# Layer 1 weights fetched a step ahead, squares added by two engines, and dense bias tables in a two-layer hybrid attention kernel

## The chip, the cores and the metric

The kernel runs on one core of a Trainium2 chip. The time is device time in microseconds (us) of one launch, as the median over several runs. The engines are TensorE (PE), VectorE (DVE), ScalarE (ACT), GpSimd (POOL) and SyncE (SP), which here issues nearly all DMAs. "SPq" in a row is SP's DMA queue, where a row stands for the issue of a transfer, not for its landing.

## What is computed

One sample with 1024 latent tokens (a 16 x 64 grid) and 256 context tokens goes through two layers of width 1024. Each layer is attention and a SwiGLU network, each behind a modulated RMS norm (scale and shift come from the conditioning vector, `ada_params`). Layer 0 attends with eight heads in a neighbourhood with a table of relative position biases, and with eight grouped-query heads; layer 1 uses differential attention.

```python
def rms_norm(x, gain=None):
    y = xf * lax.rsqrt(jnp.mean(xf * xf, axis=-1, keepdims=True) + EPS)
def ada_params(cond, w, b):
    m = jax.nn.silu(cond) @ w + b
    return jnp.split(m[..., None, :], N_MOD, axis=-1)
# neighbourhood attention of layer 0, per grid row
s_win = einsum('bhqd,bhrqjd->bhqrj', q_r, k_win) * scale + bias
s_ctx = einsum('bhqd,bhkd->bhqk', q_r, kc) * scale
# differential attention of layer 1
s1 = einsum('bhqd,bhkd->bhqk', a1, k1) * scale
s2 = einsum('bhqd,bhkd->bhqk', a2, k2) * scale
p = softmax(s1) - lam * softmax(s2)
# feed-forward
(silu(h @ w_gate) * (h @ w_up)) @ w_down
```

## The kernel before

Activations lie transposed, features on the partitions, in eight tiles of 128 features, and in three blocks of tokens: block 0 is the context (256), blocks 1 and 2 hold 512 latent tokens each. Every product is three matmuls (`mm3`, L181 to L183): both operands are split into a high and a low part (hh, hl for activations, wh, wl for weights), and high x high, low x high and high x low are summed in PSUM. A weight chunk of 128 x 1024 is fetched by SP (L171), its high part is cast by ACT (L172), and its low part is the difference, on POOL or DVE (L173).

The order of instructions on each engine is set by a scheduler from the order of the code; `high_priority` moves work ahead, and `later()` gives work the lowest priority, so that it fills what others leave. Each engine runs its own list strictly in order, and SP issues its DMAs in order too: a transfer that waits for a buffer holds those behind it.

The stages that matter here:

- **Layer 0's projections** (up to 405 us). Eight chunks of query and key weights (ch 0 to 7) are multiplied; meanwhile the row maxima of the scores that the softmax needs are taken (L432 matmul, L410 reduction from PSUM; L471 transposes the result). Beside that, a modulation vector is built: `ada_acc` fetches eight 512 KB pieces of `ada_w` (L207) and accumulates them on DVE (L210, L214), and `ada_sum` sums over the partitions with eight one-column matmuls for each of two conditions (L235; the trace records each twice). Beside that too, `tables` builds the bias tables of the neighbourhood heads: it fetches rows of the padded bias (L630), adds a mask on POOL (L631) and stores to DRAM (L634). The stored rows have a pitch of 127, and the attention reads them back skewed, in pieces of 64 floats.
- **Layer 0's attention**: S^T matmuls (L853, L854), exponentials, and value matmuls (L888 to L891).
- **Down projection of layer 0 and the norm into layer 1**: the last group of SwiGLU products is added to x on DVE (L993); ACT squares x (L322), POOL adds the squares up (L323), a matmul with ones sums over the partitions (L329), and `norm_apply` makes the products x * rstd (L343, DVE), the scale and shift (L344, ACT) and the split (L164, ACT and L165, DVE).
- **Layer 1's projections** (1990 to 2500 us): for four groups g, first the keys (kind 1), then the queries (kind 0), each with two weight chunks w1 and w2. In the code both are fetched at the head of their step. After each step sixteen stores put the rotated keys or queries into DRAM (L1211; ks, qs). Then come the V weights (L1221). In between runs the "far" part: pairs of matmuls (L1063, L1064) for the log-sum-exp of the scores, each with a DVE maximum (L1065) and an ACT exponential (L1066); its q and k are fetched back from qs and ks (L1095 to L1102). How many pairs are put between the projection matmuls is set by `far`.

Of the kernel before, what the change touches and what calls it, by code (L numbers as in the profile page):

```python
# [17 lines left out]
P = 128  # L18
D = 1024
KD = 8  # L20
# [6 lines left out]
RPW = 127  # L27
RPN = 15 * RPW
# [24 lines left out]
def kernel(ctx: ExitStack, tc: tile.TileContext, xT, cond, ada_w, ada_b, win0, wv0, wout0, rp, rpf, qg, kg,  # L53
# [78 lines left out]
    sk = [dram([8, 64 * RPN + 2048], f"sk{i}") for i in range(2)]  # L132
# [18 lines left out]
    def skew(i, h, dr0, n):  # L151
        o = 63 + dr0 * RPW
        v = sk[i][h, o : o + 64 * (RPN - 1)].rearrange("(c n) -> c n", c=64)
        return v[:, : n * RPW].rearrange("c (u y) -> c u y", y=RPW)[:, :, :GW]

# [11 lines left out]
    def load_w(src, view=None, eng=None):  # L167
        raw = wpool.tile([P, 1024], F32, tag="wl", bufs=5, name=nm("wr"))
# [7 lines left out]
    def load_wchunk(src, eng=None):  # L176
        hi, lo = load_w(src, eng=eng, view=("p (k m) -> p k m", dict(k=KD)))
        return hi.rearrange("p (k m) -> p k m", k=KD), lo.rearrange("p (k m) -> p k m", k=KD)
# [146 lines left out]
    def norm_rstd(pool, ssq, w, pstag, tb=None):  # L325
        pst = ps(*pstag)
        parts = ssq if isinstance(ssq, list) else [ssq]
        for i, x in enumerate(parts):
            nc.tensor.matmul(pst[:, :w], ones, x, start=i == 0, stop=i == len(parts) - 1)  # L329
# [155 lines left out]
    with sbuf("hp0", 8) as hp, sbuf("a10", 8) as ap:  # L485
# [134 lines left out]
        cmt = ap.tile([P, 2, RPW], F32, tag="cmt", bufs=1, name="cmt")  # L620

        def tables(i, h):

            for d0, d1 in ((0, 8), (8, 15)):
                n = d1 - d0
                T = ap.tile([P, 8, RPW], F32, tag="aw", bufs=3, name=nm("sk"))[:, 0:n, :]
                T2 = T.rearrange("p u y -> p (u y)")
                for j in range(2):
                    src = (rpf, rp)[i][h + j : h + j + 1, d0 * RPW : d1 * RPW].to_broadcast([64, n * RPW])
                    nc.sync.dma_start(T2[64 * j : 64 * j + 64], src)  # L630
                nc.gpsimd.tensor_add(T, T, cmt[:, i : i + 1, :].to_broadcast([P, n, RPW]))  # L631
                for j in range(2):
                    dst = sk[i][h + j, : 64 * RPN].rearrange("(c n) -> c n", c=64)[:, d0 * RPW : d1 * RPW]
                    nc.sync.dma_start(dst, T2[64 * j : 64 * j + 64])  # L634

# [79 lines left out]
        for ch in range(8):  # L715
# [756 lines left out]
```

## Time and profile before

| quantity | value |
|---|---|
| median of 3 runs | 3656.18 us (3655.86 to 3661.64) |
| profiled execution | 3658.97 us, of it the span 3657.2 us |
| PE busy | 3415.5 us, 93% of the span |
| DVE busy | 2218.4 us, 61% |
| ACT busy | 1422.3 us, 39% |
| POOL busy | 825.2 us, 23% |
| DMA | 394.51 MB, 198081 packets, 57692 of them under 512 B |

The profile records each instruction of one execution. A wait is the idle time of an engine ahead of an instruction, with the instruction that ended it. The granted clock is the share of TensorE's full clock (2.4 GHz) that it ran at: 0.5 is the lower level, 1.2 GHz. Where two matmuls stand next to each other, the distance of their starts is the cost, since the second begins before the first one's recorded end.

### The profile page before, as it was taken

The page shows a single profiled execution, that of the slowest core. Times are in us where ns is not written, and L with a number is a line of the kernel's source. Part 1 is how long each engine was busy: PE and PEld are TensorE (multiplying, and loading weights), DVE is VectorE, ACT ScalarE, POOL GpSimd, SP SyncE. Part 2 cuts the span into 40 slices and gives each one's busy share as a digit, 9 for nine tenths or more (in the row PEclk, how much of TensorE's full clock was granted, in tenths as well). Part 3 has the DMA queues.
Part 4 walks back from the last instruction along what each step waited for, and adds up shares of the span by engine and source line. Part 5 has one row for each costly group of instructions (what it writes and reads, how often), then busy time and mean ns, then how long its engine had stood idle before and what let it go on. Part 6 is the DMA issues. An engine that isn't in the chain of part 4 may idle for free.

```text
span 3657.2 us, 43706 instructions
## 1 busy us (share of the span) xinstructions
PE 3415.5 (93%) x16044; PEld 2783.9 (76%) x16044; DVE 2218.4 (61%) x3555; ACT 1422.3 (39%) x2862; POOL 825.2 (23%) x622
## 2 busy tenths in 40 slices
PE   6799699988999999999998899899999999999997
PEld 4588577766888888888886678787666888888886
DVE  7767388887755555554336366787998533433335
ACT  4431067666441111111115254797777421111112
POOL 3212177766220000000003322002332200000002
PEclk8899789999999999999999999999999999999999
DMA  5276764374413333231112553646442211111111
GB/s 212 78 241 223 219 136 103 87 142 97 165 52 98 104 104 98 93 98 47 35 41 87 135 140 100 201 149 189 125 127 91 98 47 50 49 53 47 47 47 64
DMA packets 198081, 394.51 MB, mean 108 GB/s; under 512 B 57692, under 2 KB 99216, under 8 KB 197866
## 3 DMA queue, kind: packets, MB, share of 16 engines
q1 hardware_dynamic: 196074, 388.62, 36.0%
q0 software_dynamic: 1792, 3.10, 0.2%
q8 instruction: 126, 2.06, 0.2%
q14 instruction: 89, 0.73, 0.1%
HBM read 317.03 MB, written 74.61 MB: 107 GB/s over the span
## 4 chain that ended last, share of the span: by engine, by line
PE 74%; DVE 10%; ACT 5%; POOL 3%; issue 3%; DMA 3%; SPq 1%; POOLq 0%; DVEq 0%; ACTq 0%
PE psd L181 6%; PE psd L182 6%; PE psd L183 6%; PE psg L181 5%; PE psg L182 5%; PE psg L183 5%; PE psu L183 4%; PE psu L181 4%; PE psu L182 4%; PE psm L183 4%; PE psm L182 4%; PE psm L181 4%; PE pst L1318 2%; PE psq L1063 2%; PE pst L1319 2%
## 5 line engine op out<-in xcount | busy, mean ns | idle before, releaser
L173 POOL TENSOR_TENSOR wl<-wr,wh 128x1024 fp32r<-128x1024 f32 x69 | 168.0, 2435 | 1521.7 <-ACT wh L172 1315.4
L172 ACT CAST wh<-wr 128x1024 fp32r<-128x1024 f32 x193 | 202.2, 1049 | 761.7 <-PE psd L182 305.7
L993 DVE SCALAR_TENSOR_TENSOR x<-psd,mods,x 128x512 f32<-128x512 f32 (+1 forms) x448 | 301.3, 686 | 190.7 <-PE psd L183 190.4
L1027 DVE TENSOR_TENSOR sg<-sg,psu 128x512 f32<-128x512 f32 (+1 forms) x110 | 69.6, 634 | 484.4 <-PE psu L183 477.9
L181 PE MATMUL psd<-ah,wh 128*128 128x512 f32 (+1 forms) x896 | 331.3, 370 | 8.8 <-DVE x L993 6.8
L182 PE MATMUL psd<-al,wh 128*128 128x512 f32 (+1 forms) x896 | 328.3, 366 | 0.0
L183 PE MATMUL psd<-ah,wl 128*128 128x512 f32 (+1 forms) x896 | 326.9, 366 | 0.8 <-DVE wl L173 0.7
L181 PE MATMUL psg<-hh,wh 128*128 128x512 f32 (+1 forms) x880 | 326.2, 371 | 0.9 <-ACT sg L1024 0.9
L183 PE MATMUL psg<-hh,wl 128*128 128x512 f32 (+1 forms) x880 | 325.3, 370 | 0.1
L182 PE MATMUL psg<-hl,wh 128*128 128x512 f32 (+1 forms) x880 | 325.0, 369 | 0.0
L183 PE MATMUL psu<-hh,wl 128*128 128x512 f32 (+1 forms) x880 | 323.8, 368 | 0.5 <-POOL wl L173 0.5
L181 PE MATMUL psu<-hh,wh 128*128 128x512 f32 (+1 forms) x880 | 324.1, 368 | 0.0
L182 PE MATMUL psu<-hl,wh 128*128 128x512 f32 (+1 forms) x880 | 323.6, 368 | 0.0
L173 DVE TENSOR_TENSOR wl<-wr,wh 128x1024 fp32r<-128x1024 f32 x124 | 156.0, 1258 | 220.7 <-ACT wh L172 204.8
L1065 DVE TENSOR_REDUCE st<-psq 128x1 f32<-128x512 f32 (+1 forms) x384 | 219.4, 596 | 58.3 <-PE psq L1064 53.5
L1066 ACT ACTIVATE psq<-psq,st 128x512 f32<-128x512 f32 (+1 forms) x384 | 226.8, 594 | 65.0 <-DVE st L1065 61.3
L181 PE MATMUL psm<-hh,wh 128*128 128x512 f32 (+1 forms) x584 | 219.2, 376 | 25.7 <-ACT wh L172 18.4
L849 POOL TENSOR_TENSOR pl<-sb,ph 128x512 fp32r<-128x512 f32 (+1 forms) x144 | 203.5, 1420 | 91.9 <-ACT ph L848 60.2
L182 PE MATMUL psm<-hl,wh 128*128 128x512 f32 (+1 forms) x584 | 217.4, 373 | 6.5 <-DVE hl L349 4.7
L183 PE MATMUL psm<-hh,wl 128*128 128x512 f32 (+1 forms) x584 | 217.9, 373 | 3.7 <-POOL wl L173 3.7
L181 PEld LDWEIGHTS psd<-ah,wh 128*128 128x128 f32 x896 | 169.4, 189 | 44.0 <-DVE x L993 13.5
L1024 ACT ACTIVATE sg<-psg 128x512 f32<-128x512 f32 (+1 forms) x110 | 60.5, 552 | 344.4 <-PE psg L183 344.4
(276 smaller groups left out, 8331.2 us busy)
## 6 DMA issues: line engine op xcount, KB each, us to landing
aw<-in_ada_w SPq DMA_DIRECT2D x112, 512.0 KB
wr<-in_wg SPq DMA_DIRECT2D x44, 512.0 KB
wr<-in_wu SPq DMA_DIRECT2D x44, 512.0 KB
wr<-in_wd SPq DMA_DIRECT2D x44, 512.0 KB
k<-ks SPq DMA_DIRECT2D x32, 640.0 KB
wr<-in_wout SPq DMA_DIRECT2D x32, 512.0 KB
q<-qs SPq DMA_DIRECT2D x32, 512.0 KB
k<-ks SPq DMA_DIRECT2D x48, 320.0 KB
```

The lines of the kernel that those rows point to most:

```text
L172: nc.scalar.copy(hi, raw)
L173: (eng or nc.gpsimd).tensor_sub(lo, raw, f(hi))
L181: nc.tensor.matmul(o, ah, bh, start=start, stop=False)
L182: nc.tensor.matmul(o, ah, bl, start=False, stop=False)
L183: nc.tensor.matmul(o, al, bh, start=False, stop=stop)
L849: (nc.vector if npb[0] % LOD == 0 else nc.gpsimd).tensor_sub(lo, e, f(hi))
L993: nc.vector.scalar_tensor_tensor(xv, pst, mods[:, l, ci, 40 + oc : 41 + oc], xv, op0=ALU.mult, op1=ALU.add)
L1063: nc.tensor.matmul(p1, q2[:, a * P : a * P + P], k2[:, k0 : k0 + kw], start=True, stop=False)
L1065: nc.vector.tensor_reduce(st[:, 0, a, j : j + 1], p1, axis=AX.X, op=ALU.max, negate=True)
L1066: after_table(nc.scalar.activation(p1, p1, AF.Exp, bias=st[:, 0, a, j : j + 1], accum_out=st[:, 1, a, j : j + 1]))
L1318: nc.tensor.matmul(o, ks[c][1][:, kk], qs[c][1][:, c0 : c0 + 512], start=True, stop=False)
L1319: nc.tensor.matmul(o, ks[c][0][:, kk], qs[c][0][:, c0 : c0 + 512], start=False, stop=True)
```

## The change

- `load_w` takes a raw buffer from outside; in the down projection the raw buffers of a group are taken before the first load.
- In layer 0, the bias tables come in dense from the host (`tabT`, `tabQ`: rows of 15 x 64 for each of the 64 grid columns). `tables` is now one load, one POOL add of 960 columns and one store for two heads, where it was two pieces with two loads and two stores each. The attention reads contiguous rows.
- In layer 0's projections, the last `ada_acc` no longer stands under `later()`, and its sum comes at chunk 6 where it was at chunk 4.
- In the norm into layer 1 and in the last norm, every other square addition goes to DVE (`nc.vector if oc % 2 else None`).
- The ones matmul of block 2 gets a lower priority (`behind=70`).
- The first two weight chunks of layer 1 are fetched in the last down projection (`first_w`); after that each step fetches the next step's w1 at its head and the next step's w2 in its middle, and the last step fetches the first V weights (`vw1`).

```diff
-        raw = wpool.tile([P, 1024], F32, tag="wl", bufs=5, name=nm("wr"))
+    def load_w(src, view=None, eng=None, raw=None):
+        raw = wpool.tile([P, 1024], F32, tag="wl", bufs=5, name=nm("wr")) if raw is None else raw
...
+    def norm_rstd(pool, ssq, w, pstag, tb=None, behind=0):
...
+            with tc.high_priority(-behind):
+                nc.tensor.matmul(pst[:, :w], ones, x, start=i == 0, stop=i == len(parts) - 1)
...
-            for d0, d1 in ((0, 8), (8, 15)):
-                n = d1 - d0
-                T = ap.tile([P, 8, RPW], F32, tag="aw", bufs=3, name=nm("sk"))[:, 0:n, :]
...
+            T = ap.tile([P, 15, GW], F32, tag="aw", bufs=3, name=nm("sk"))
+            r = slice(64 * h, 64 * h + P)
+            nc.sync.dma_start(T.rearrange("p u y -> p (u y)"), (tabT, tabQ)[i][r])
+            nc.gpsimd.tensor_add(T, T, cmt[:, i : i + 1, :].to_broadcast([P, 15, GW]))
+            nc.sync.dma_start(sk[i][r], T.rearrange("p u y -> p (u y)"))
...
-            if ch in (1, 4):
+            if ch in (1, 6):
                 ada_sum(*pend_ada, qmt)
             if ch == 1:
-                with later():
-                    pend_ada = ada_acc(ap, *adas.pop(0))
+                pend_ada = ada_acc(ap, *adas.pop(0))
...
+            if l == 0:
+                first_w.append(load_wchunk(win1[8], nc.vector))
+                first_w.append(load_wchunk(win1[9], nc.vector, fp.tile([P, NT], F32, tag="al", bufs=4, name="wr1")[:, :1024]))
...
-                    sumsq_add(fp, sv, one(oc, blk), oc == 0, ("ah", NT, 4))
+                    sumsq_add(fp, sv, one(oc, blk), oc == 0, ("ah", NT, 4), nc.vector if oc % 2 else None)
...
-                rstd = norm_rstd(fp, sv, w, S1, 4)
+                rstd = norm_rstd(fp, sv, w, S1, 4, 70 if b == 2 else 0)
...
-                        w1 = load_wchunk(win1[kind * 8 + 2 * g], None if g or not kind else nc.vector)
-                        w2 = load_wchunk(win1[kind * 8 + 2 * g + 1], None if g or not kind else nc.vector)
+                        w1, w2 = ws
+                        nxt = order1[2 * g + 2 - kind] if 2 * g + 2 - kind < 8 else None
+                        ws = [load_wchunk(win1[nxt])] if nxt is not None else []
+                        if nxt is None:
+                            vw1(0, 0)
...
+                            if b == (0 if kind else 2):
+                                if nxt is not None:
+                                    ws.append(load_wchunk(win1[nxt + 1]))
+                                else:
+                                    vw1(0, 2)
...
-                for k0 in range(0, KD, 2):
...
+                for k0 in range(4 * (1 - g), KD, 2):
+                    vw1(g, k0)
```

How this moves instructions is seen in the order of each engine. PE, end of layer 0's projections, before (`psm` are projections, `acc` the modulation, `km`, `qm` the maxima's operands):

```order
L182 MATMUL psm_3628<-hl_538,wh_3533 128x512
L183 MATMUL psm_3628<-hh_537,wl_3532 128x512
L235 MATMUL psq_3216<-cst,acc_2710 128x1 x8
L432 MATMUL psq_3268<-km_1342,qm_2877 128x512
L432 MATMUL psq_3271<-km_1342,qm_2877 128x256
L235 MATMUL psq_3216<-cst,acc_2711 128x1 x8
L432 MATMUL psq_3274<-km_1342,qm_2877 128x512
```

Behind these follow 49 more L432 and two L471, and then the first S^T matmul. The same place after the change:

```order
L179 MATMUL psm_3564<-hl_538,wh_3469 128x512
L180 MATMUL psm_3564<-hh_537,wl_3468 128x512
L430 MATMUL psq_3589<-km_1342,qm_3287 128x512
L430 MATMUL psq_3592<-km_1342,qm_3287 128x256
L430 MATMUL psq_3595<-km_1342,qm_3287 128x512
L430 MATMUL psq_3598<-km_1342,qm_3287 128x512
L430 MATMUL psq_3601<-km_1342,qm_3287 128x256
L430 MATMUL psq_3604<-km_1342,qm_3287 128x512
L430 MATMUL psq_3607<-km_1342,qm_3287 128x512
L430 MATMUL psq_3668<-km_1342,qm_3287 128x256
L430 MATMUL psq_3671<-km_1342,qm_3288 128x512
L844 MATMUL pst_3675<-t_714_3653,t_716_3659 128x256
```

Nine maxima stand between the last projection matmul and the first S^T matmul (L844); the modulation sums and the other maxima have moved up among the projections.

SP, layer 1, between the key stores and the query stores of group 1 (`wr` is a weight; the second one is w2 of group 2's keys), after the change:

```order
L1232 DMA ks_93<-t_3177_16822 32x1280
L168 DMA wr_17051<-in_win 128x1024
L1232 DMA qs_92<-t_3206_17057 32x1024
L1232 DMA qs_92<-t_3207_17058 32x1024
L168 DMA wr_17226<-in_win 128x1024
L1232 DMA qs_92<-t_3208_17059 32x1024
L1232 DMA qs_92<-t_3209_17060 32x1024
```

The second weight stands behind two of the query stores. In group 0 (first weight of the next step, then the stores) it stands ahead of them, after the change:

```order
L1232 DMA ks_93<-t_3131_16448 32x1280
L168 DMA wr_16753<-in_win 128x1024
L1232 DMA qs_92<-t_3152_16659 32x1024
L1232 DMA qs_92<-t_3153_16660 32x1024
```

Before, the same weight (w2 of group 1's keys) stood behind all sixteen, and this is the end of them:

```order
L1211 DMA qs_92<-t_3160_16719 32x1024
L1211 DMA qs_92<-t_3161_16720 32x1024
L171 DMA wr_16871<-in_win 128x1024
```

DVE, the norm into layer 1, the end of block 2's squares, before (no square addition on DVE; `x` is the result of the last down projection, `na` the products and `hl` the splits of block 1):

```order
L343 TENSOR_TENSOR na_16271<-x_8451,rs_16250 128x512
L993 SCALAR_TENSOR_TENSOR x_8456<-psd_16388,mods,x_8456 128x512
L165 TENSOR_TENSOR hl_16259<-na_16257,hh_16258 128x512
L165 TENSOR_TENSOR hl_16266<-na_16264,hh_16265 128x512
L343 TENSOR_TENSOR na_16278<-x_8452,rs_16250 128x512
```

and after:

```order
L985 SCALAR_TENSOR_TENSOR x_8392<-psd_16336,mods,x_8392 128x512
L162 TENSOR_TENSOR hl_16207<-na_16205,hh_16206 128x512
L162 TENSOR_TENSOR hl_16214<-na_16212,hh_16213 128x512
...
L341 TENSOR_TENSOR na_16247<-x_8391,rs_16198 128x512
L341 TENSOR_TENSOR na_16254<-x_8392,rs_16198 128x512
L162 TENSOR_TENSOR hl_16242<-na_16240,hh_16241 128x512
L320 TENSOR_TENSOR ssq_15938<-ssq_15938,sq_16344 128x512
```

The last square addition (L320) stands twelve instructions behind the last x. On PE the ones matmul of block 2 stands at the same place in both orders, ahead of layer 1's first projection matmul.

## Rows read from the trace of the kernel before

**Rows 1.** PE's waits, whole span: line, what it waited for, us, times, longest.

```profile
PE psq L235 <- DVE acc L214: 38.2, 3, 33.7
PE psm L181 <- ACT wh L172: 18.4, 3, 14.5
```

**Rows 2.** Windows, layer 0: stretch, length, busy (instructions) by engine, PEclk, DMA share, GB/s.

```profile
core 0: us, PE busy (x) PEld busy (x) DVE busy (x) ACT busy (x) POOL busy (x), PEclk, DMA share, GB/s
280.00:405.00 125.00, 124.23 (x640) 106.01 (x638) 74.18 (x124) 15.28 (x28) 31.73 (x17) 0.97 0.73 224
405.00:475.00 70.00, 33.65 (x92) 22.55 (x91) 46.18 (x73) 1.12 (x3) 11.59 (x15) 0.53 0.73 209
```

**Rows 3.** PE timeline, 398 to 480: start, us, instruction, count [idle before <- releaser].

```profile
404.70 0.39 PE L182 MATMUL psm<-hl,wh 128*128 128x512 f32 x1
404.93 0.39 PE L183 MATMUL psm<-hh,wl 128*128 128x512 f32 x1
439.01 3.57 PE L235 MATMUL psq<-cst,acc 128*128 128x1 f32 x16 [33.69 <-DVE acc L214]
...
474.25 0.41 PE L853 MATMUL pst<-t,t 128*128 128x256 f32 x1
```

**Rows 4.** SP's DMA queue, timeline 280 to 475: issues.

```profile
416.00 17.27 SPq L207 DMA_DIRECT2D aw<-in_ada_w  x8
...
463.95 1.93 SPq L784 DMA_DIRECT2D v<-vs  x2
```

**Rows 5.** Groups on DVE by shape, 280 to 475: count | busy, mean ns | idle.

```profile
L410 DVE TENSOR_REDUCE mx<-psq 128x1 f32<-128x512 f32 x82 | 53.6, 685 | 6.9 <-PE psq L432 6.5
L214 DVE SCALAR_TENSOR_TENSOR acc<-aw,cs,acc 128x1024 f32<-128x1024 f32 x28 | 35.3, 1326 | 0.2 <-DMA aw<-in_ada_w 0.2
L410 DVE TENSOR_REDUCE mx<-psq 128x1 f32<-128x256 f32 x41 | 17.0, 414 | 2.9 <-PE psq L432 2.8
```

**Rows 6.** PE timeline, the norm into layer 1.

```profile
1990.24 2.08 PE L329 MATMUL pss<-ssq,cst 128*128 128x512 f32 x2 [8.57 <-POOL ssq L323]
```

**Rows 7.** DVE timeline, the norm into layer 1.

```profile
1981.67 5.53 DVE L343 TENSOR_TENSOR na<-x,rs 128x512 f32<-128x512 f32 x3
1987.13 0.74 DVE L993 SCALAR_TENSOR_TENSOR x<-psd,mods,x 128x512 f32<-128x512 f32 x1
...
1991.97 0.69 DVE L343 TENSOR_TENSOR na<-x,rs 128x512 f32<-128x512 f32 x1
```

**Rows 8.** Windows, layer 1's projections, columns as in rows 2.

```profile
2052.00:2075.00 23.00, 7.29 (x20) 5.01 (x19) 1.89 (x3) 1.17 (x2) 2.35 (x1) 0.63 0.88 245
2160.00:2194.00 34.00, 27.26 (x109) 18.42 (x109) 20.30 (x46) 21.47 (x66) 7.63 (x4) 0.90 0.72 201
2284.00:2300.00 16.00, 6.94 (x21) 4.51 (x19) 3.94 (x5) 3.35 (x4) 0.00 (x0) 0.68 0.97 260
2320.00:2500.00 180.00, 180.00 (x856) 145.91 (x856) 155.46 (x346) 166.56 (x537) 5.58 (x10) 1.00 0.49 155
```

**Rows 9.** SP's DMA queue, timeline, layer 1's projections.

```profile
2050.15 11.42 SPq L1211 DMA_DIRECT2D qs<-t  x16
2061.66 0.55 SPq L171 DMA_DIRECT2D wr<-in_win  x1
...
2277.32 10.71 SPq L1211 DMA_DIRECT2D qs<-t  x16
```

**Rows 10.** PE timeline, second key weight of group 1.

```profile
2067.22 0.80 PE L181 MATMUL psm<-hh,wh 128*128 128x512 f32 x1 [14.50 <-ACT wh L172]
...
2069.65 0.79 PE L183 MATMUL psm<-hh,wl 128*128 128x512 f32 x1 [1.21 <-POOL wl L173]
```

**Rows 11.** The page's groups, whole span: busy, mean ns of one | idle before.

```profile
L172 ACT CAST wh<-wr 128x1024 fp32r<-128x1024 f32 x193 | 202.2, 1049 | 761.7 <-PE psd L182 305.7
```

**Rows 12.** Groups on ACT by shape, 2000 to 2300, columns as in rows 5.

```profile
L1066 ACT ACTIVATE psq<-psq,st 128x512 f32<-128x512 f32 x80 | 53.0, 665 | 39.6 <-DVE st L1065 38.7 <-DVE st L1073 0.4
L1066 ACT ACTIVATION_READ_ACCUMULATOR psq<-psq,st 128x1 f32 x120 | 24.2, 202 | 0.0
L1066 ACT ACTIVATE psq<-psq,st 128x256 f32<-128x256 f32 x40 | 18.0, 451 | 10.5 <-DVE st L1065 10.3
...
L164 ACT CAST t<-rp 128x512 fp32r<-128x512 f32 x16 | 9.9, 620 | 28.8 <-POOL rp L370 22.2 <-POOL rp L371 6.6
```

More of the change, by code (lines that the diff above doesn't have):

```diff
@@ L131 @@
     onesrow = dram([2, NT], "onesrow")
-    sk = [dram([8, 64 * RPN + 2048], f"sk{i}") for i in range(2)]
+    sk = [dram([8 * 64, 15 * GW], f"sk{i}") for i in range(2)]
     def small_operands():
@@ L619 @@
                 gqa_q(g, w1, w2, o, blk)
-        cmt = ap.tile([P, 2, RPW], F32, tag="cmt", bufs=1, name="cmt")
+        cmt = ap.tile([P, 2, GW], F32, tag="cmt", bufs=1, name="cmt")
         def tables(i, h):
-            for d0, d1 in ((0, 8), (8, 15)):
-                n = d1 - d0
-                T = ap.tile([P, 8, RPW], F32, tag="aw", bufs=3, name=nm("sk"))[:, 0:n, :]
[L627 to L634, printed above, removed]
+            T = ap.tile([P, 15, GW], F32, tag="aw", bufs=3, name=nm("sk"))
[3 more added lines that the diff above has]
+            nc.sync.dma_start(sk[i][r], T.rearrange("p u y -> p (u y)"))
         mpool = None
@@ L983, in down @@
         def down(group, last):
-            ws = [load_w(wd[l, ci], eng=nc.vector) for ci, _, _ in group]
+            raws = [wpool.tile([P, 1024], F32, tag="wl", bufs=5, name=nm("wr")) for _ in group]
+            ws = [load_w(wd[l, ci], eng=nc.vector, raw=r) for r, (ci, _, _) in zip(raws, group)]
             def one(oc, blk):
@@ L1173, with vw1 @@
             done = 0
+            vwt = ([], [])
+            def vw1(g, k0):
+                lo = wpool.tile([P, 1024], F32R, tag="wl", bufs=5, name=nm("vwl"))
+                hi = wpool.tile([P, 1024], F32R, tag="wh", bufs=4, name=nm("vwh"))
+                raw = t5(ap, F32)[:, :1024]
+                lov = lo.rearrange("p (k c) -> p k c", k=2)
+                hiv = hi.rearrange("p (k c) -> p k c", k=2)
+                nc.sync.dma_start(raw.rearrange("p (k c) -> p k c", k=2),
+                                  wv1[k0 : k0 + 2, :, g * 512 : g * 512 + 512].rearrange("k p c -> p k c"))
+                split_hi(hi, lo, raw)
+                for k in range(2):
+                    vwt[g].append((hiv[:, k, :], lov[:, k, :]))
             def far(t):
@@ L1213 @@
             for g in range(2):
[L1214 to L1225 removed]
+                for k0 in range(4 * (1 - g), KD, 2):
+                    vw1(g, k0)
+                wt = vwt[g]
                 for t in range(10):
@@ L1409 @@
     rp = np.pad(inp["na_rpb"][0], ((0, 0), (0, 0), (48, 48)))
+    x = GW - 1 - np.arange(GW)[:, None] + np.arange(GW)[None, :]
+    tabQ, tabT = (t[:, :, x].transpose(0, 2, 1, 3).reshape(8 * GW, 15 * GW) for t in (rp, rp[:, ::-1, ::-1]))
     qgain, kgain = inp["gqa_q_gain"][0], inp["gqa_k_gain"][0]
@@ L1425 @@
     inside = (c[None, :] >= start[:, None]) & (c[None, :] < start[:, None] + 16)
[L1427 to L1432 removed]
+    mq = np.where(inside, f32(0), f32(NEG)).astype(f32)
+    cmT, cmQ = np.concatenate([mq.T, mq.T], axis=0), np.concatenate([mq, mq], axis=0)
     arrays = dict(
```

37 lines of the change are left out of this document (8 added, 29 removed).

## Prediction

> **What bounds the kernel now.** TensorE (PE) is the engine with by far the most busy time (the table above), so what a change can win is PE's idle time and the slow clock behind each idle stretch. The first view is therefore the list of PE's waits, longest first. Its two longest lines are places that the diff touches [rows 1]: 38.2 us, of which 33.7 in one piece, in which PE waits for an accumulation on VectorE (L214), and 18.4 us (14.5 in one piece) in which it waits for the ACT cast of a weight (L172). For each place I then read the windows around it (busy time and granted clock), the timeline of PE, and the timeline of SyncE's DMA queue, to see whether the transfer was late because it was slow or because it was issued late. Both times it is the issue: the eight loads for the 33.7 us go out from 416.00 on, after the projections have ended at 405.3 [rows 3, 4], and the weight behind the 14.5 us is issued at 2061.66, right behind sixteen stores that hold SP from 2050.15 on [rows 9].
>
> The sum is made against the profiled execution, 3659.0 us; the median of the runs shown is 3656.2, which is 2.8 less, and the forecast is brought to that at the end.
>
> **Part 1: the end of layer 0's projections.** The last projection matmul starts at 404.93, the first S^T matmul of the attention at 474.25 [rows 3]. In between lie the one-column matmuls of the modulation sums (L235, 32 records), 52 matmuls of the row maxima (L432) and two transposes. PE is busy 33.65 of the 70 us, at a granted clock of 0.53, that is mostly the 1.2 GHz level; from 280 to 405 it was 0.97, nearly always 2.4 GHz [rows 2]. After the change the accumulation no longer has the low priority: its loads stand in SP's queue in the middle of the projections, both modulation sums stand among the projection matmuls of the last two chunks, and 43 of the 52 maxima stand between matmuls of earlier chunks. Nine are left at the end.
>
> What remains behind 405.3: the 43 maxima at the full clock cost 0.23 each (the distance of the two matmul starts at 404.70 and 404.93 [rows 3]), 9.9 us; 32 tiny matmuls at about 0.1 (half of 3.57/16 at the half clock [rows 3]), 3.4; the nine maxima left at VectorE's pace, 0.57 (the mean over the two forms, 53.6 + 17.0 over 123 [rows 5]), 5.2. That puts the first S^T at 405.3 + 18.5 = 423.8, so 50.4 us earlier. Can VectorE carry it? From 280 to 405 it is busy 74.2 of 125 us [rows 2]; sixteen accumulations at 1.33 [rows 5] and 43 reductions at 0.57 add 21.3 + 24.7, together 120 of the 138 us up to 419, or 87%. It works in program order with few PSUM buffers between, so some stalls are to come: up to 8 us. The other end: if PE's new work falls into gaps that it had (0.8 us in that stretch) and the nine are hidden, the S^T comes at 419. If the operands of the first head come late (the V tiles were issued only at 463.95 [rows 4], behind the tables, and now stand between the operands of the first and the second head), 440. I take **50 us**, with 34 (the long wait alone) and 55 as the ends. After the first S^T both programs have the same matmuls in nearly the same order, so the gain stays.
>
> The tables: one add of 960 columns in place of two of 1016 and 889 (x 2 halves of the partitions), half the bytes, and the same queue. These lie beside PE work before and after: 0. They take 8 stores of SP and POOL time out of the stage, which is part of why the loads can be early.
>
> **Part 2: the norm between the layers.** PE ends the last down projection at 1981.7 and waits 8.57 us for the last addition of squares on POOL, until 1990.24 [rows 6]. The cause is VectorE's order: the last x (L993) starts only at 1987.13, behind three products of block 1's norm, 5.53 us for three, or 1.84 each, while POOL is adding; one such product took 0.69 at 1991.97, with POOL idle [rows 7]. The change gives every other square addition to VectorE, and in VectorE's new order the last one stands not behind three products but behind all eight, and behind six of the eight splits: twelve instructions after the last x. At 0.69 each and from 1987.8 on these reach to 1996.1, and the addition itself to 1996.8. With fewer additions POOL disturbs the first three products less, by up to 3 x 1.15, so the other end is 1993.3. Nearer to the middle: the ones matmul of block 2 starts at about 1995 instead of 1990.2, a **loss of 4.5 us**. For the range I take 0 (a product that isn't disturbed anywhere else either) to 9 (four of the products behind the last x at 1.84). The argument `behind=70` doesn't move this matmul: it stands ahead of layer 1's first projection in both orders, so what is late there stays in front. The first two weights of layer 1 were already fetched beside the last SwiGLU group before, so that edit is worth 0. The Trainium skill, GPSIMD Engine Reference, section Key points, says that GpSimd shares its SBUF interfaces with VectorE, and that they contend when a VectorE instruction has two SBUF inputs; that speaks against giving both engines square additions at the same time. The trace agrees (1.84 against 0.69); by it the four additions new to VectorE would take 1.15 more each, 4.6 us together, and the forecast would be 3603, inside this term's range.
>
> **Part 3: layer 1's projections.** What the stalls cost before, as the length of a window less its matmuls at the full clock (0.2275 each): 23 - 20 x 0.2275 = 18.4 at group 1's keys (2052 to 2075), 34 - 109 x 0.2275 = 9.2 at group 2's (2160 to 2194), 16 - 21 x 0.2275 = 11.2 at the first V weights (2284 to 2300) [rows 8]. Together 39 us; this holds the half clock behind the waits.
>
> After the change, by the order on SP: group 1's second key weight stands ahead of the query stores, so this wait goes: 18.4 won. For groups 2 and 3 the second key weight stands behind the first two of the sixteen query stores. When does SP get there? In group 0 the first query store goes out at 2050.15 [rows 9]; PE had then begun group 1's first key weight 5.5 us (24 matmuls) before its wait at 2067.22 - 14.50 = 2052.7 [rows 10], that is at 2047.2. So stores begin 2.9 us behind the end of the queries, and the weight is issued two stores later (2 x 0.71, 11.42/16 [rows 9]), at 4.3. From issue to its first matmul took 5.56 (2061.66 to 2067.22), 1.05 of it the cast [rows 11]. That makes 9.9 us, less the 5.5 of the 24 matmuls: a wait of 4.4, and 1.2 more for its low half, as before [rows 10]; with half clock behind it (18.4 less the two waits, 15.7, is 2.7 for the long one; 1.7 for these shorter ones) 7.3 each. So groups 2 and 3 lose 14.6, where group 2 alone lost 9.2. Of the V weights' four pieces two stand ahead of the stores; the other two have the 48 matmuls of the first two (11 us) and the softmax sums between them to hide behind, against 10.71 us of stores; 3 left.
>
> A cost that the diff doesn't name: the loads of q and k for the "far" softmax sums (L1095 on) now come behind the weights and the stores, so these pairs of matmuls bunch. In the new order 45 pairs fall on the 96 projection matmuls from the 624th to the 720th (23 before), and 24 on the 48 from the 960th (5 before). One pair costs ACT (2 x 0.665 + 0.451)/3 + 0.202 = 0.80 us [rows 12]; PE (2 x 0.455 + 0.23)/3 = 0.38. The first bunch needs 36 us of ACT plus about 15 casts and rope steps at 0.62 [rows 12], 45 us, against PE's 39; the second, with seven of the casts, 23.5 against 20: about 9.5 together. Later, in the window 2320 to 2500, ACT is busy 166.6 of 180 [rows 8], so what is left over there isn't caught up by being earlier. Bounds: 0 and 15. I take 9.
>
> Part 3 in sum: 39 - 14.6 - 3 - 9 = **12 us won** (from 0 to 39).
>
> **Elsewhere.** Last norm at the end: 11 additions go from POOL to VectorE, which is nearly full there; between -2 and +2, taken as 0. The feed-forward order is the same but for the order in which buffers are given.
>
> Sum: 50 - 4.5 + 12 = 57.5; 3659.0 - 57.5 = 3601.5, and on the scale of the median **3598 us**.
>
> **Rivals.** *A: VectorE and the transfers take the place of the wait in part 1.* For it: VectorE at 87%, a DMA share of 0.73 in the projections [rows 2], and V tiles that stand behind them. Against it: PE was 99% busy there while VectorE was 59% and DMA 73% busy. Then only 34 of the 50 are won: 3614. *B: the layer 1 weights come in time everywhere and the sums don't bunch on the path.* For it: the scheduler may start stores later than I read, and the softmax sums have free ACT time around. Against it: the position of the loads behind two stores. Then all 39 us are won: 3598 - 27 = 3571. *C: the change does not do what it says in layer 1*: the ones matmul stays in front, the first weights were early anyway, and the later groups' waits (14.6) and bunches (15) eat what group 1 wins; with a norm loss of 9 the sum is 50 - 9 + 3 = 44: 3612. *D, the slower side: head-of-line waiting on VectorE.* The accumulations now stand in the middle of VectorE's queue, each pair of them behind its own 512 KB load; when a load is late, all maxima and evacuations behind it stand, and PE after its few PSUM buffers. Sixteen loads are moved forward (two modulations). It decides against the change when each holds VectorE for more than 57.5/16 = 3.6 us; before, eight such loads went out in 17.27 us [rows 4], 2.2 each with the accumulations that free their buffers, so it would have to be almost twice that with nothing hidden: at 4.1 each 65.6 us, and 3664.
>
> **How the numbers follow.** Chances: forecast 0.50, A 0.17, B 0.12, C 0.17, D 0.04. The range runs from 3570 (B) to 3620 (A with a norm loss of 9, rounded up), leaving out D and the tails. Faster by over 0.2% (7 us, about what a measurement of this kernel can tell from no change): all but D and a little, 0.94; the same 0.02; slower 0.04.
>
> **What would show it.** Part 1: no wait of PE over 5 us between 400 and 430, the clock near 1.0 there, and the first S^T at 419 to 432. Part 2: the ones matmul 12 to 17 us behind the last down matmul instead of 8.6. Part 3: no wait at group 1's second key weight, two waits of about 6 us for ACT casts (L169) at groups 2 and 3, and the softmax sums of layer 1 bunched with ACT near full. The forecast is wrong if the S^T starts after 440, or if groups 2 and 3 show no wait.

## The result, and the profile after

The changed kernel takes 3617.8 us as the median of four runs (3616.9 to 3619.3), beside 3658.7 for the kernel before in the same session; the ratio is 0.9889 with a 95% interval of 0.9871 to 0.9906. That is 41 us or 1.1% faster. The forecast was 3598, its range 3570 to 3620.

The page of the changed kernel, its busy times and its packets:

```profile
span 3616.0 us, 43603 instructions
PE 3398.5 (94%) x16044; PEld 2775.9 (77%) x16044; DVE 2216.1 (61%) x3579; ACT 1415.7 (39%) x2862; POOL 792.3 (22%) x590
DMA packets 160449, 386.70 MB, mean 107 GB/s; under 512 B 19036, under 2 KB 60560, under 8 KB 160234
```

PE does the same 16044 matmuls; 37,600 packets are gone (160449 against 198081), and the count under 512 B fell by 38,656. PE's waits over the whole span answer [rows 1]:

```profile
PE pss L327 <- DVE ssq L320: 17.4, 3, 14.0
...
PE psm L178 <- ACT wh L169: 15.7, 3, 8.0
...
PE psm L180 <- POOL wl L170: 11.1, 8, 1.7
PE psq L430 <- DVE mx L408: 10.7, 12, 3.5
...
PE psm L178 <- ACT vwh L161: 7.2, 3, 5.5
...
PE psq L232 <- DVE acc L211: 4.2, 2, 2.9
```

The wait for the accumulation fell from 38.2 to 4.2 us. The wait for weight casts hardly fell at all, from 18.4 to 15.7, and a line for the low halves on POOL (L170), 11.1 us in eight pieces, is new near the top.

Cut at four matmuls that both programs have, the two profiled executions give this table (differences of start times on PE):

| stretch | before, us | after, us | difference |
|---|---|---|---|
| start to the first S^T of layer 0 | 474.3 | 431.6 | -42.7 |
| to the ones matmul of block 2, norm into layer 1 | 1516.0 | 1517.9 | +1.9 |
| to the first score matmul of layer 1's attention | 520.1 | 521.7 | +1.6 |
| to the end of the span | 1146.9 | 1144.8 | -2.1 |

So all of the gain lies in layer 0's projections. The windows there answer [rows 2]:

```profile
280.00:405.00 125.00, 118.29 (x587) 99.12 (x586) 99.55 (x160) 14.94 (x28) 27.57 (x20) 0.95 0.55 194
405.00:431.50 26.50, 25.75 (x141) 21.27 (x139) 13.34 (x30) 2.40 (x5) 1.31 (x3) 1.00 0.82 221
```

DVE is busy 99.6 of the 125 us where it was 74.2, PE is at 118 instead of 124, and behind 405 PE runs at the full clock. On PE's timeline the first S^T answers the last of [rows 3]; the longest new wait in the projections is one for a maximum:

```profile
354.60 0.38 PE L430 MATMUL psq<-km,qm 128*128 128x256 f32 x1 [3.46 <-DVE mx L408]
...
431.58 0.39 PE L844 MATMUL pst<-t,t 128*128 128x256 f32 x1
```

In the norm into layer 1 the ones matmul answers [rows 6]; the second row is where layer 1's projections lose time:

```profile
1949.50 2.07 PE L327 MATMUL pss<-ssq,cst 128*128 128x512 f32 x2 [14.01 <-DVE ssq L320]
...
2074.06 0.80 PE L178 MATMUL psm<-hh,wh 128*128 128x512 f32 x1 [6.28 <-ACT wh L169]
2076.74 0.79 PE L180 MATMUL psm<-hh,wl 128*128 128x512 f32 x1 [1.46 <-POOL wl L170]
...
2162.05 0.80 PE L178 MATMUL psm<-hh,wh 128*128 128x512 f32 x1 [7.98 <-ACT wh L169]
```

The wait of 14.50 at group 1's second key weight ([rows 10]) is gone (groups are counted from 0). In its place stand two waits at the first key weights of groups 2 and 3, 6.28 and 7.98. The sums of PE's waits in layer 1's projections, counted between the ones matmul and the first score matmul, are nearly the same: 36.0 us before and 37.4 after.

### The profile page after: what moved, and what is told of

Same layout as the page of the kernel before. It is cut to its first block, busy times and chain, and to the rows that moved or that the text cites. A ratio compares the mean times of both kernels' runs of the same rounds, so it can differ in the third digit from the quotient of the medians.

```text
span 3616.0 us, 43603 instructions
## 1 busy us (share of the span) xinstructions
PE 3398.5 (94%) x16044; PEld 2775.9 (77%) x16044; DVE 2216.1 (61%) x3579; ACT 1415.7 (39%) x2862; POOL 792.3 (22%) x590
## 2 busy tenths in 40 slices
DMA packets 160449, 386.70 MB, mean 107 GB/s; under 512 B 19036, under 2 KB 60560, under 8 KB 160234
## 3 DMA queue, kind: packets, MB, share of 16 engines
q1 hardware_dynamic: 158442, 380.81, 35.3%
## 5 line engine op out<-in xcount | busy, mean ns | idle before, releaser
L170 POOL TENSOR_TENSOR wl<-wr,wh 128x1024 fp32r<-128x1024 f32 x69 | 168.9, 2449 | 1505.6 <-ACT wh L169 1132.1
L169 ACT CAST wh<-wr 128x1024 fp32r<-128x1024 f32 x193 | 202.1, 1048 | 725.8 <-PE psd L179 307.5
L170 DVE TENSOR_TENSOR wl<-wr,wh 128x1024 fp32r<-128x1024 f32 x124 | 155.5, 1254 | 217.1 <-ACT wh L169 201.1
L1061 ACT ACTIVATE psq<-psq,st 128x512 f32<-128x512 f32 (+1 forms) x384 | 225.9, 590 | 61.2 <-DVE st L1060 59.3
L178 PE MATMUL psm<-hh,wh 128*128 128x512 f32 (+1 forms) x584 | 219.2, 376 | 22.2 <-ACT wh L169 15.7
L180 PE MATMUL psm<-hh,wl 128*128 128x512 f32 (+1 forms) x584 | 218.6, 375 | 11.1 <-POOL wl L170 11.1
```

Of the source, the lines that this page charges most:

```text
L169: nc.scalar.copy(hi, raw)
L170: (eng or nc.gpsimd).tensor_sub(lo, raw, f(hi))
L178: nc.tensor.matmul(o, ah, bh, start=start, stop=False)
L180: nc.tensor.matmul(o, al, bh, start=False, stop=stop)
L1061: after_table(nc.scalar.activation(p1, p1, AF.Exp, bias=st[:, 0, a, j : j + 1], accum_out=st[:, 1, a, j : j + 1]))
```

## The experiments

Every kernel was timed beside the kernel before, in four or five runs (e4 in eleven); the changed kernel itself was timed once more beside the second group (a1): 3618.3 us.

| run | what it is | median, us | ratio to before, 95% interval |
|---|---|---|---|
| a1 | the changed kernel again | 3618.3 | 0.9885 (0.9871 to 0.9898) |
| e1 | layer 1's fetches put back | 3610.8 | 0.9872 (0.9859 to 0.9886) |
| e2 | squares put back on POOL | 3612.8 | 0.9874 (0.9859 to 0.9889) |
| e3 | accumulation put back to the lowest priority | 3612.7 | 0.9870 (0.9857 to 0.9884) |
| e4 | tables put back | 3666.8 | 1.0024 (1.0015 to 1.0032) |
| e13 | before, with the dense tables alone | 3608.4 | 0.9855 (0.9842 to 0.9869) |
| e15 | before, dense tables in the old pieces | 3626.8 | 0.9901 (0.9888 to 0.9915) |
| e5 | changed, priority for the next w1 | 3598.2 | 0.9838 (0.9825 to 0.9851) |
| e8 | changed, priority for both next weights | 3597.9 | 0.9827 (0.9812 to 0.9841) |
| e10 | e5 with the squares on POOL | 3597.7 | 0.9829 (0.9816 to 0.9843) |
| e11 | e8 with e3 | 3589.7 | 0.9804 (0.9790 to 0.9817) |
| e14 | e11 with priority for the V weights | 3592.3 | 0.9813 (0.9799 to 0.9826) |

### One part put back at a time: e1, e2, e4, e3

**e1** puts the weight fetches of layer 1 back (`w1` and `w2` at the head of their step, no `first_w`, no `vw1`):

```diff
-                        w1, w2 = ws
...
-                        ws = [load_wchunk(win1[nxt])] if nxt is not None else []
...
+                        w1 = load_wchunk(win1[kind * 8 + 2 * g], None if g or not kind else nc.vector)
+                        w2 = load_wchunk(win1[kind * 8 + 2 * g + 1], None if g or not kind else nc.vector)
```

> The changed kernel, with the weight fetches of layer 1 put back as they were (both weights at the head of their step, V weights behind the stores). Theory 1, from the two traces: between the first ones matmul of block 2 and the first scores of layer 1's attention the changed kernel needs 521.7 us and the kernel before 520.1, and the waits of TensorE in that stretch sum to 37 and 36 us; the one wait of 14.5 has turned into waits of 6.3 and 8.0 for the ACT cast of the next step's first weight and into seven of 1 to 1.7 for the low halves on POOL. So the fetches are worth nothing: 3616 +- 4 us. Theory 2, the prediction on record: the fetches win 12 us, so putting them back costs 12: 3630.

3610.8 us: neither. The fetches don't win 12 us and aren't worth 0 either, they cost about 7. Its trace agrees: 514.5 us from the ones matmul to the first score matmul, where the changed kernel needs 521.7. The old long wait is back (15.7 us). The windows over this stretch, e1 first, then the changed kernel:

```profile
1951.40:2465.90 514.50, 478.70 (x2226) 386.81 (x2226) 341.16 (x664) 315.13 (x916) 84.05 (x65) 0.96 0.51 144
1949.50:2471.20 521.70, 482.75 (x2226) 388.27 (x2226) 335.38 (x664) 308.25 (x916) 84.38 (x65) 0.96 0.51 142
```

The same 2226 matmuls leave PE idle 35.8 us in e1 and 39.0 in the changed kernel, and they are recorded as 4 us longer in the latter. So 3 of the 7 us are waits; where the other 4 come from is not shown. The loss lies ahead of the V weights: e1's first V matmul starts 283.7 us behind the ones matmul, with 120 of the 384 softmax pairs done, the changed kernel's at 286.5 with 96. The 24 missing pairs are 9.1 us of PE at 0.38 each, so the changed kernel is 12 us behind there, and wins 5 back behind it, where PE idles 4.2 us and in e1 10.1.

**e2** puts all squares back on POOL:

```diff
-                    sumsq_add(fp, sv, one(oc, blk), oc == 0, ("ah", NT, 4), nc.vector if oc % 2 else None)
+                    sumsq_add(fp, sv, one(oc, blk), oc == 0, ("ah", NT, 4))
```

> The changed kernel, with all square additions on POOL again. Theory 1, from the traces: the ones matmul of block 2 waited 14.0 us instead of 8.6, but the splits of block 1 are ready by then and no longer hold the first projection, so that at the end of the first step the loss is only 0.5 us; the last norm won about 1. Then the time is 3617 to 3621, and the wait is back at 8 to 9 us. Theory 2, the prediction on record: the two engines cost 4.5 us, so this kernel is at 3613.

3612.8 us, as the prediction on record had it by number. The ones matmul of block 2 waits again as before:

```profile
1942.98 2.07 PE L327 MATMUL pss<-ssq,cst 128*128 128x512 f32 x2 [8.57 <-POOL ssq L320]
```

But the trace doesn't put the 5 us there. From the first S^T to the first score matmul of layer 1 e2 needs 2040.0 us and the changed kernel 2039.6: the ones matmul's wait is 5.4 us shorter, and 5.0 are lost again in the first 144 projection matmuls (35.1 us against 30.1), where in e2 the matmuls wait for the splits. Only 2 us lie behind that, at the last norm; the rest of the 5.1 is a first S^T that came 3.6 us earlier, in a stage whose order is the same in both. See e10.

**e4** puts the tables back as they were (pitch 127, two pieces, short reads), with everything else of the change kept:

> The changed kernel, with the bias tables as before (pitch of 127, two pieces, pieces of 64 floats read back). Theory 1: the tables lie beside TensorE's work, but the dense reads are why layer 0's attention and feed-forward network won 3.5 us beyond the 42.7 of the projections; and with twice the stores on SP's queue the accumulation's loads come later again: 5 to 12 us slower than the changed kernel, 3623 to 3630. Theory 2, the prediction on record: 0, so 3618.

3666.8 us: 49 slower than the changed kernel and even slower than before (ratio 1.0024, 1.0015 to 1.0032). Both theories are wrong by far. Without the dense tables the priority of the accumulation still brings the first S^T forward, to 450.29 from 474.25, 24.0 us; but from there to the ones matmul e4 needs 1548.5 us, 32.5 more than before, and all is lost again. The rows of e4, PE's waits, its first S^T, and then SP's queue:

```profile
PE psq L236 <- DVE acc L215: 25.4, 3, 20.9
...
PE pst L854 <- ACT sb L844: 13.7, 3, 13.1
...
450.29 0.41 PE L854 MATMUL pst<-t,t 128*128 128x256 f32 x1
```

```profile
411.55 1.85 SPq L208 DMA_DIRECT2D aw<-in_ada_w  x2
...
423.64 3.58 SPq L208 DMA_DIRECT2D aw<-in_ada_w  x2
...
476.91 1.87 SPq L785 DMA_DIRECT2D v<-vs  x2
478.82 4.44 SPq L810 DMA_DIRECT2D TQ<-sk  x1
```

The accumulation's last loads still go out at 423.64, in the midst of operands, although they no longer have the lowest priority, and PE waits 20.9 us for them. And what moved ahead of the tables made these later: the V tiles are issued at 476.91 and the query tables at 478.82. The 13.1 us are waited at 478.95, behind the first S^T matmuls, for exponentials on ACT; these wait for the probabilities' low halves (`pl`), and POOL's timeline shows what holds those up:

```profile
471.64 4.11 POOL L633 TENSOR_TENSOR sk<-sk,cmt 128x1016 f32<-128x1016 f32 x2 [7.99 <-issue]
...
477.01 4.95 POOL L850 TENSOR_TENSOR pl<-sb,ph 128x512 fp32r<-128x512 f32 x4
```

The additions of the tables' last pieces (L633) stand ahead of the low halves (L850) in POOL's order, and POOL stands idle for 8 us before them, their loads having been issued only at 465.

**e3** keeps the dense tables and puts the accumulation back:

```diff
-            if ch in (1, 6):
+            if ch in (1, 4):
                 ada_sum(*pend_ada, qmt)
             if ch == 1:
-                pend_ada = ada_acc(ap, *adas.pop(0))
+                with later():
+                    pend_ada = ada_acc(ap, *adas.pop(0))
```

> The changed kernel, with the accumulation back at the lowest priority and its sum at chunk 4; the tables stay dense. Theory 1, after the run in which the tables alone were put back and the time rose to 3667: the tables' transfers are what the accumulation's loads waited behind, so the dense tables alone free them, and the order of SP's queue already shows the eight loads in the middle of the projections: within 10 us of the changed kernel, 3612 to 3628. Theory 2, the prediction on record: the priority is what moves the loads, so without it the wait of 33.7 us comes back: 3650 or more.

3612.7 us, all four runs (3611.8 to 3613.5) below all four of a1 (3614.7 to 3620.3). So with the dense tables the priority that I took for the cause of 50 us costs about 5 (together with the later place of its sum, which this edit moves back too), and theory 1 is right. PE waits less for maxima from 300 to 435 us, first in e3, then in a1:

```profile
PE psq L430 <- DVE mx L408: 1.9, 3, 1.3
```

```profile
PE psq L430 <- DVE mx L408: 5.5, 5, 3.4
```

The other traces agree: these waits sum to 5.5 to 6.5 us in all seven executions with the priority (after, a1, e1, e2, e5, e8, e10), and to 1.9 in all three changed kernels without it (e3, e11, e14).

### The tables alone: e13 and e15

**e13** is the kernel before with only the dense tables (the part of the diff from `sk` to `tables`).

> The kernel before, with the dense tables alone, and none of the other edits. Theory 1, from the four runs that put one part back (tables: 3667, accumulation: 3613, fetches: 3611, squares: 3613, changed kernel: 3618): the tables carry the whole gain, and the other edits cost together 5 to 15 us: 3602 to 3612. Theory 2, the prediction on record: the tables are worth 0 and the priority of the accumulation wins the 50 us: 3655 to 3662.

3608.4 us. Theory 1 holds: one edit alone gives more than the whole change, 3617.8. The first S^T comes at 426.97, 47.3 us earlier than before, and the other three stretches are as before within 0.1, 0.5 and 3.1 us. The accumulation still has the lowest priority here, yet its loads go out from 318.5 to 363.5, where before they went out from 416.00. A window, PE's first S^T and SP's queue of e13 beside [rows 2, 3, 4]:

```profile
405.00:475.00 70.00, 67.03 (x312) 52.42 (x311) 56.24 (x101) 38.55 (x73) 37.28 (x33) 1.00 0.67 184
...
426.97 0.38 PE L843 MATMUL pst<-t,t 128*128 128x256 f32 x1 [0.68 <-DVE mx L406]
```

```profile
318.49 0.33 SPq L203 DMA_DIRECT2D aw<-in_ada_w  x1
...
337.81 12.18 SPq L203 DMA_DIRECT2D aw<-in_ada_w  x4
359.65 3.87 SPq L203 DMA_DIRECT2D aw<-in_ada_w  x2
373.63 0.33 SPq L622 DMA_DIRECT2D sk<-in_tabT  x1
```

So the other edits of the change together cost about 9 us. Put back singly they gave 7 (e1), 5 (e3) and 0 to 5 (e2, e10); the raw buffers and `behind=70` had no run of their own.

**e15** asks what of the tables it is: the dense bytes, or the number of transfers. It builds the dense tables in the old two pieces, with four loads and four stores where e13 has one of each, and twice as many turns of the three `aw` buffers that tables and accumulation share:

```diff
-            T = ap.tile([P, 15, GW], F32, tag="aw", bufs=3, name=nm("sk"))
...
+            for d0, d1 in ((0, 8), (8, 15)):
+                n = d1 - d0
+                T = ap.tile([P, 8, GW], F32, tag="aw", bufs=3, name=nm("sk"))[:, 0:n, :]
...
+                for j in range(2):
+                    r = slice(64 * (h + j), 64 * (h + j) + 64)
+                    nc.sync.dma_start(T2[64 * j : 64 * j + 64], (tabT, tabQ)[i][r, d0 * GW : d1 * GW])
...
```

> The kernel before, with the dense tables, but built in the two pieces and four loads and stores of before (64 floats wide where it was 127): half the bytes and dense reads, yet as many transfers on SP's queue, and as many turns of the three buffers that the tables share with the accumulation. Theory 1: the number of transfers and buffer turns is what held the accumulation: its wait stays, in part at least, and the time is 3630 to 3655. Theory 2: the bytes and the short pieces are what it was: as fast as the dense tables in one piece, within 5 us.

3626.8 us: between the two theories, nearer to the second. Of the 53 us that e13 wins over the kernel before in the same session (3661.7), 35 come from the bytes and the dense reads, and 18 from making each table in one piece; fewer transfers and fewer buffer turns go together here, and the run doesn't separate them. e15's first S^T is as early as e13's (427.07), so the number of transfers is not what held the accumulation; but its V tiles and tables are late behind the remaining pieces, and it loses 15.4 us from there to the ones matmul. SP's queue of e15, where e13 issues the V tiles at 415.43:

```profile
439.13 1.74 SPq L630 DMA_DIRECT2D sk<-sk  x3
440.92 1.82 SPq L780 DMA_DIRECT2D v<-vs  x2
```

### Where layer 1's gain went: e5, e8, e10, e11, e14

In the changed kernel the first key weight of group 2 is issued at 2041.18, more than 30 us before it is needed. ACT's timeline shows why it still was late:

```profile
2069.72 1.15 ACT L374 ACTIVATE t<-rp 128x512 fp32r<-128x512 f32 x2 [0.46 <-POOL rp L368]
2071.18 0.63 ACT L374 ACTIVATE t<-rp 128x512 fp32r<-128x512 f32 x1 [0.31 <-POOL rp L369]
2072.18 0.22 ACT L1067 ACTIVATE st<-st 128x24 f32<-128x24 f32 x1 [0.37 <-DVE st L1066]
2072.87 0.21 ACT L1070 ACTIVATE sv<-sv 128x8 f32<-128x8 f32 x1 [0.46 <-DVE sv L1069]
2072.98 1.03 ACT L169 CAST wh<-wr 128x1024 fp32r<-128x1024 f32 x1
2076.11 1.04 ACT L169 CAST wh<-wr 128x1024 fp32r<-128x1024 f32 x1 [2.10 <-DMA wr<-in_win]
```

The cast (L169, at 2072.98) has no idle time of its own: it runs the moment ACT has finished the rope (L374) and the end of a softmax sum (L1067, L1070), and PE stands from 2067.8 to 2074.06. The second weight's cast behind it does wait for its transfer.

**e5** gives the fetch and the cast of the next step's w1 a higher priority:

```diff
-                        ws = [load_wchunk(win1[nxt])] if nxt is not None else []
+                        with tc.high_priority(400):
+                            ws = [load_wchunk(win1[nxt])] if nxt is not None else []
```

> The changed kernel, with a higher priority for the fetch and the cast of the next step's first weight. The load keeps its place behind the key stores on SP's queue; the cast moves on ACT's queue from behind the rope and the softmax sums of the query step to its beginning. Theory 1: the waits at groups 2 and 3 (6.3 + 1.5 and 8.0 + 1.3 us, with the half clock behind them) are the cast's place on ACT's queue, since the weight had landed some 25 us earlier: they go, and the time is 3600 to 3606. Theory 2: the weight lands late or SP issues it late; then the waits stay or turn into waits of ACT, and the time is 3614 to 3620.

3598.2 us, 20 below the changed kernel: theory 1, and a little more. (The load did not keep its place, as the expectation says; it moved ahead of the key stores, to 2032.39, and the cast ran at 2036.5. So the run shows that the place in the queues was the cause, and doesn't separate the two queues.) The waits left at groups 2 and 3 are now those for the second weight:

```profile
2073.91 0.50 PE L178 MATMUL psm<-hh,wh 128*128 128x512 f32 x1 [1.86 <-ACT wh L169]
2076.40 0.77 PE L180 MATMUL psm<-hh,wl 128*128 128x512 f32 x1 [1.75 <-POOL wl L170]
...
2154.28 0.50 PE L178 MATMUL psm<-hh,wh 128*128 128x512 f32 x1 [2.15 <-ACT wh L169]
```

**e8** gives the second weight the same priority (one more `with tc.high_priority(400)` around its fetch).

> The changed kernel, with a higher priority for the fetch and the cast of both weights of the next step (with the first alone it took 3598.2 us, and two waits of 1.9 and 2.2 us for the second weight's cast were left, with 1.8 and 0.6 for its low half). Theory 1: these go too, about 8 us with the clock: 3588 to 3594. Theory 2: the weights in front push back the stores, and these the loads of the softmax sums, which bunch more and are paid later: 3596 to 3602.

3597.9 us, no better than e5 in the median: theory 2's number, but not its reason. In the trace layer 1's projections do gain, 492.7 us against 503.8 in e5. Of these 11 us 3.9 are lost ahead of them, between the first S^T and the ones matmul (1525.1 us against 1521.2): the weights' low halves now run on POOL in the middle of the norm, and the ones matmul of block 2 waits 18.2 us instead of 14.0. The profiled executions differ by 4.4 us (3597.8 and 3602.2), with a first S^T that happens to come 1.8 us later in e8, and four runs each, 3591.7 to 3599.6 and 3595.9 to 3604.0, don't tell the two apart.

**e10** is e5 with the squares on POOL (the edit of e2).

> The changed kernel, with the higher priority for the next step's first weight, and all squares on POOL. Theory 1: the two engines cost 2 to 5 us (the run with the squares on POOL alone was 5.1 below the changed kernel, 2 of it visible behind the first scores of layer 1), so it is at 3593 to 3596. Theory 2: the splits of block 1 hold the first projection instead, and there is no difference to the 3598.2 of the priority alone: 3597 to 3600.

3597.7 us against 3598.2: theory 2. The step of e2 that the trace could not place doesn't come back. So what the two engines cost or win in these norms is between 0 and 5 us; e2 and e10 disagree, and it stays open.

**e11** is e8 with the accumulation at the lowest priority (the edit of e3).

> The changed kernel, with the accumulation back at the lowest priority (alone 3612.7) and the higher priority for both weights of the next step (alone 3597.9). Theory 1: the two gains lie in different stages and add up: 3590 to 3594. Theory 2: they don't: 3596 to 3600.

3589.7 us: the gains of e3 and e8 add up (8.1 below e8), and this is the fastest kernel here, 2.0% below the kernel before (ratio 0.9804, 0.9790 to 0.9817) and 28 us below the changed kernel.

**e14** adds the same priority for the first V weights, here and for the second `vw1` call:

```diff
-                            vw1(0, 0)
+                            with tc.high_priority(400):
+                                vw1(0, 0)
...
```

> As the kernel with the accumulation at the lowest priority and both weights at the higher one, and the higher priority for the first V weights too, of which the last third step's end still waits 5.5 us in the changed kernel. Theory 1: this wait goes with the clock behind it, 4 to 8 us below the kernel without it: 3583 to 3589. Theory 2: the pairs of softmax sums that come later take it up: no difference.

3592.3 us, five runs from 3587.5 to 3597.6: no difference from e11 that these runs can tell, so theory 2's side. The wait for V casts wasn't removed, and in sum it is longer: 11.9 us in four pieces in its trace, 7.3 in three in that of e11.

## Why the prediction was right or wrong

**The range held, and the size was off by 20 us.** The sum had three terms: 50, -4.5 and 12. The table of stretches gives 42.7 for the first; -1.9 up to the ones matmul and -1.6 for what follows, where the second and the third together had 7.5; and 2.1 for the end, taken as 0. That the range held is luck: its largest term named the wrong edit, parts 2 and 3 lost 3.5 where they were to win 7.5, and the time lies 2.2 us inside the upper bound.

**Part 1: right size, wrong cause.** The step that failed is "The tables ... These lie beside PE work before and after: 0". It asked only whether POOL and the transfers of the tables are hidden at the moment at which they run. It didn't ask what stands behind them on SP's in-order queue and in the `aw` buffers that they share with the accumulation, although in the trace before the accumulation's loads, at 416.00 [rows 4], follow right behind these stores of the tables:

```profile
413.95 2.00 SPq L634 DMA_DIRECT2D sk<-sk  x3
```

e13 gives the tables 47.3 us in this stage with no other edit. Without them the priority brings 24.0 us at the first S^T, half of the 50, and the attention behind gives them back (e4); with them it costs 5 (e3). The diff removes `later()`, and I took the edit that names the waiting instruction for the one that frees it. Whether the dense tables free the loads through SP's queue or through the buffers, no run separates; e15 shows that it is not the number of transfers. The signs that the prediction named for this part (no wait over 5 us, full clock, S^T by 432) came true and couldn't tell the two causes apart.

The working itself held in size: the forecast put the S^T at 423.8, and at 432 with all of the 8 us of stalls; it came at 431.6. Stalls there were: the waits for maxima that "VectorE at 87%" foresaw, 6.0 us, and e3 shows that most of them came from the moved accumulation: they are 1.9 us without the priority. Rival A's 16 us were twice what was lost: 50 forecast, 42.7 measured. Rival D, accumulations ahead of maxima in VectorE's queue, is this same effect; it cost 5 us and not the 57.5 that it would have needed.

**Part 2: right at its place, and of no effect where it was counted.** The ones matmul waited 14.0 instead of 8.6, 5.4 more, where 4.5 were forecast. What failed is that the term was put into the sum whole. The time it delays was already lost: before, and in e2, the first 144 projection matmuls waited for the splits and took 35.1 us; with the splits ready they take 30.1. The loss left at their end is 0.5 us. The stretch from the first S^T to the ones matmul is only 1.9 us longer in spite of the 5.4; what won the other 3.5 no run shows.

VectorE's and POOL's timelines have three products beside POOL's work, two while POOL is idle, and the last square additions:

```profile
1934.57 4.48 DVE L341 TENSOR_TENSOR na<-x,rs 128x512 f32<-128x512 f32 x3
1941.49 1.28 DVE L341 TENSOR_TENSOR na<-x,rs 128x512 f32<-128x512 f32 x2
1944.12 4.60 POOL L320 TENSOR_TENSOR ssq<-ssq,sq 128x512 f32<-128x512 f32 x1 [5.62 <-DVE ssq L320]
1948.75 0.69 DVE L320 TENSOR_TENSOR ssq<-ssq,sq 128x512 f32<-128x512 f32 x1 [1.17 <-POOL ssq L320]
```

The Trainium skill's contention between the two engines (GPSIMD Engine Reference, Key points) is seen in the rows here as well: three products took 4.48 us beside POOL, and two 1.28 without it. Later POOL is the one that pays: its last addition took 4.60 us beside VectorE's row of products and splits, where the two before took 1.29 and 1.61, and VectorE's own last addition waited 1.17 us for it.

**Part 3: the wait went, the gain didn't.** Of the 18.4 us forecast at group 1, 16.6 are won: measured by the matmul count, the step behind group 1's keys comes 62.3 us earlier than before, where group 1's keys themselves begin 45.7 us earlier. Two steps failed behind that.

- "For groups 2 and 3 the second key weight stands behind the first two of the sixteen query stores" is right about SP, and e5 shows the waits that follow from it: 1.9 and 1.8, 2.2 and 0.6 us, where 4.4 and 1.2 were worked out. But in the changed kernel the step stops one weight earlier, at the first one, whose cast stands on ACT's queue behind rope and softmax sums: 6.3 and 8.0 us. I looked up the place of the load on SP and not the place of the cast on ACT; the order of ACT would have shown it. That the price, 7.3 each, came out near the measured one is chance.
- The bunching of the softmax pairs came as read from the order (48 pairs between the 624th and the 720th matmul, 45 forecast; 24 and 24 in the second bunch), but the price of 9 us for ACT's extra time isn't shown. ACT is busy 35.3 us of the 55.4 of the first bunch, not near full, and PE's waits for ACT's exponentials (L1061) are 3.0 us in the whole kernel:

```profile
2106.60:2162.00 55.40, 43.60 (x196) 33.25 (x194) 37.12 (x76) 35.31 (x109) 11.63 (x8) 0.96 0.31 76
```

New and not in the sum are the waits for the low halves on POOL, eight with 11.1 us, where before there were three with 3.7. A low half takes POOL 2.4 us behind its cast, and where the cast is just in time the low half comes late; in e5, with the first weight earlier, there are five with 5.3. The stretch of part 3 is 1.6 us longer than before, though its first 144 matmuls are 5.0 shorter (part 2). So what lies behind them lost 6.6 us in place of the 12 won, as e1 says by its time. This is what rival C described (the later groups' waits and the bunches eat what group 1 wins), and it had 17% of the chance; its number, 3612, and rival A's, 3614, are the nearest to 3617.8.

## What to carry to other kernels

Before an edit gets a price, ask for each transfer it removes which instructions stand behind it on the same in-order queue and in the same rotating buffers: that, and not whether the transfer itself is hidden, decided over 47 us here. A fetch one step ahead is only as early as the latest of its steps: look up the place of the load on the issuing queue, of the cast, and of the difference, each on its own engine. And put parts back one at a time: of the edits one carried the gain and two cost time (the squares stay open), and without the runs all would have been kept.

## What the runs showed that was not expected

Two prices of the tables came apart: with the bytes halved and the reads dense, but the number of table transfers and buffer turns kept, 35 of 53 us were won (e15); the other 18 came with a quarter of the transfers and half of the turns (e13).

Identical orders of layer 0 gave first S^T matmuls from 428.0 to 434.4 us in seven profiled executions (after, a1, e1, e2, e5, e8, e10: 431.6, 433.8, 433.7, 428.0, 432.6, 434.4, 431.5). Differences of 2 to 5 us between two kernels are therefore only told where several runs of each agree; without the priority (e3, e11, e14) it came at 424.6 to 428.3.
